# A one-core ConvFFN decoder trunk: the sync engine's loads and stores in the order of the program

## The chip, the cores and the metric

The kernel runs on one core of one Trainium2 chip. A core has a matrix engine (TensorE, "PE" in the profile, with its weight loads as "PEld"), three engines for elementwise work (VectorE "DVE", ScalarE "ACT", GpSimd "POOL"), and a sync engine "SP", which here does nothing but issue transfers. Each engine takes its instructions in one fixed order. An instruction that waits for a semaphore holds up whatever stands behind it on the same engine. Transfers run on 16 DMA engines.

The metric is the device time of one execution in microseconds (us), as the median of several runs. Lower is better.

## The reference

The trunk has two layers, on 1024 positions of 1024 channels in float32. Layer 0 mixes with convolutions, layer 1 with stick-breaking attention. Each layer ends in the gated ConvFFN, which is the part that matters here:

```python
def conv_ffn(h, w_up, dw_w, dw_b, w_down):      # w_up 1024 x 5632, w_down 2816 x 1024
    u = causal_dwconv(h @ w_up, dw_w, dw_b)     # depthwise, width 3
    gate, val = jnp.split(u, 2, axis=-1)
    return (jax.nn.silu(gate) * val) @ w_down

h = rmsnorm(x, ffn_norm_g[layer])
x = x + conv_ffn(h, ...)
```

## The kernel before

Every matrix product in it is made of three: each operand is split into a high part (a cast on ACT) and a low part (a subtraction on DVE), and `mm3` (L641) multiplies high by high, high by low and low by high. Both products of the ConvFFN also use a Strassen-like scheme with seven block products in place of eight, so that sums and differences of blocks are made first.

**Memory.** `Mem` (L48) hands out slots of 128 x 1024 float32 from one list, always the one that was freed longest ago. A transfer into a slot has to wait until every earlier user of that slot is done.

**Up-projection** (`Up`, L153). It runs over 22 blocks `f` of 128 hidden channels. `load(f)` (L174) issues three transfers from SP: half of the value weights (L182, into the slot where a sum will be made), the gate weights (L183) and the value weights (L184). `sums(f)` (L186) makes four weight sums: two negated copies on ACT (L193, L194), then four accumulating transfers from POOL (L199), of which the third reads what the first made. `split1` and `split2` (L202, L210) split weights and sums (casts L628 and L217, subtractions L629 and L218). `block(f)` (L367) starts with `load(f + 2)`, makes the products that are still missing (seven for each block, of 12 matmuls each, with copies L388, L390, L394 and L399 in between), and ends in `post(f)` (L408): the convolution (L817, L819), sigmoid (L420), two multiplications (L421, L422) and `store(f)`. `store` (L427) writes the result to scratch memory `hs`: an even block with one transfer (L434), an odd one, after four sums on DVE (L441), with three (L443). These transfers are issued by SP, but by POOL for the last two blocks.

So the order of the program on SP is: load of block 3, store of block 1, load of block 4, store of block 2, and so on. The load of block `f` stands behind the store of block `f - 3` (the loads of blocks 0 to 2 come before the loop).

**Down-projection** (`Down`, L454). It has 44 steps: four passes `s` over 11 pairs of blocks `i`. A step of the first three passes has 24 matmuls, one of the last pass 12. `load` (L479) issues the transfers of a step: rows of the down weights (L492 in the first pass, L494 in the second, L499 and L500 in the third) and the activations from `hs` (L495). `prep` (L503) makes the differences of weights (L513) and the splits (casts L517, subtractions L518; in the last pass L524 and L525). In the program, `ahead` (L548) puts a step's transfers three steps before its products and its splits two steps before. `run` (L577) also loads halves of the residual `x` (L589, 16 transfers, needed only when a pass ends), adds the products onto it (L571), and calls `tail` for finished rows. In layer 0 the tail is `tail0` (L1560), which loads the weights of the attention (L1160) and stores `x` (L1574). In layer 1 it is `store` (L1549), which writes the output (L1550): in the program, eight of its twelve transfers stand among the loads of the last pass, and four at the end.

**What sets the order.** The program only says what depends on what. The build plays the program through a model of the chip and gives each engine an order of its own, in which an instruction that is free to go may pass one that is not. Only inside `tc.manual_schedule(engines=...)` do the named engines keep the order of the program. Before the change that is used at two places, the start of the first mixer (L924) and the attention (L1454, for PE).

Of the kernel before, what the change touches and what calls it, by code (L numbers as in the profile page):

```python
# [31 lines left out]
NF = DFF // P  # L32
# [586 lines left out]
class Kern:  # L619
# [517 lines left out]
    def ffn(self, l, tail):  # L1137

        up = self.up
        self.banks = deque([b[:, c:c + 512] for b in self.bigs for c in (0, 512)] + self.sms)  # L1140
        up.turn_rest()
        down = Down(self, l, tail)
        for f in range(NF):
            up.block(f)
            if f == NF - 3:
                down.load()
            elif f == NF - 2:
                down.load()
                down.prep()
        up.close()  # L1150
        self.m.give_ht()
        down.run()


    def qkv_load(self, p):
# [466 lines left out]
```

## Time and profile before

| | |
|---|---|
| median of 3 runs | 2364.24 us (2361.4 to 2365.21) |
| the profiled execution, whole | 2360.4 us |
| its span, first to last instruction | 2358.2 us |
| mean granted TensorE clock | 0.982 |
| moved by SP's queue / by POOL's | 238.32 MB / 72.78 MB |

The four stretches that the change reaches are, by the profile's clock: the up-projection of layer 0 from about 385 to 800 us, its down-projection to about 1054 us, the up-projection of layer 1 from about 1710 to 2125 us, and its down-projection to the end.

In rows of a timeline, the columns are the start in us, the duration, engine, line, operation, what is written and read, and the count; in brackets stands the idle time before it and what ended it. SP's rows are issues, not transfers: a row with a count above one begins with the first issue and ends with the last. In the table by stretches, each engine has its busy time and, in brackets, its instructions; then come the granted clock of TensorE, the busy share of the DMA engines, and GB/s.

### The profile page before, as it was taken

Reading aid. Unit: us, or ns where it says so; the run is one execution under the profiler, and the core shown is the slowest. Engines: PE = TensorE matmul, PEld = TensorE weight load, DVE = VectorE, ACT = ScalarE, POOL = GpSimd, SP = SyncE. Lnnn points to the kernel's source line nnn. Section 1 sums busy time; section 2 is a strip of 40 time slices with the busy share of each in tenths; the row PEclk is TensorE's granted clock in tenths of the full one; section 3 lists DMA queues with packets and bytes.
Section 4 is the critical chain, followed back from the end, with each engine's and each line's share of the span. In section 5 each row is a group of like instructions: output and inputs, shape, how many; then the busy total and the mean of one; then the engine's idle time right before and its main releaser. Section 6 shows DMA issues by size and latency. Waiting matters only on the chain. (4 is left out here: it accounts for less than half of the span.)

```text
span 2358.2 us, 29782 instructions
## 1 busy us (share of the span) xinstructions
PE 2250.7 (95%) x11076; PEld 1921.4 (81%) x11076; DVE 1726.9 (73%) x2023; ACT 1263.9 (54%) x1978; POOL 561.3 (24%) x551
## 2 busy tenths in 40 slices
PE   8998999999999989999999999989999999998999
PEld 8876887888888767889999999978778888886777
DVE  6779457877777856556888888887768787786763
ACT  6433336555555423446777676764656555563341
POOL 2221111211111000025555555652221111100000
PEclk9999999999999989999999999989999999999999
DMA  5984046767676863311111110134476676769322
GB/s 173 188 169 105 29 125 148 196 152 188 153 182 164 315 226 103 117 63 28 36 28 37 37 37 10 37 115 149 122 174 159 177 175 167 184 190 391 111 76 76
DMA packets 247827, 313.01 MB, mean 133 GB/s; under 512 B 12557, under 2 KB 170753, under 8 KB 247681
## 3 DMA queue, kind: packets, MB, share of 16 engines
q1 hardware_dynamic: 214977, 238.32, 30.8%
q0 software_dynamic: 32704, 72.78, 17.3%
q8 instruction: 87, 1.43, 0.2%
q14 instruction: 59, 0.48, 0.1%
HBM read 181.14 MB, written 60.82 MB: 103 GB/s over the span
## 5 line engine op out<-in xcount | busy, mean ns | idle before, releaser
L199 POOL DMA_DIRECT2D t<-t x176 | 155.6, 973 | 699.1 <-ACT t L194 285.7
L628 ACT CAST t<-t 128x1024 fp32r<-128x1024 f32 x178 | 185.0, 1048 | 226.7 <-DMA hs<-t 53.3
L629 DVE TENSOR_TENSOR t<-t,t 128x1024 fp32r<-128x1024 f32 x178 | 218.8, 1235 | 100.4 <-ACT t L628 42.3
L819 DVE SCALAR_TENSOR_TENSOR t<-t,cst,t 128x1023 f32<-128x1023 f32 (+1 forms) x184 | 236.1, 1286 | 75.4 <-ACT t L817 69.4
L1273 DVE TENSOR_TENSOR_SCAN t<-t 128x127 f32<-128x127 f32 (+7 forms) x128 | 204.1, 1600 | 7.2 <-ACT t L1264 7.0
L644 PE MATMUL ps1s<-wH,hH 128*128 128x384 f32 x448 | 165.8, 370 | 0.0
L644 PE MATMUL ps0b<-hH,t 128*128 128x512 f32 x396 | 156.3, 396 | 2.7 <-DVE t L1104 1.5
L710 POOL TENSOR_TENSOR stat<-stat,mhalf 128x8 f32<-128x8 f32 (+1 forms) x65 | 80.1, 1233 | 322.9 <-DVE stat L709 320.0
L646 PE MATMUL ps0b<-hH,t 128*128 128x512 f32 x396 | 154.9, 392 | 1.2 <-DVE t L629 1.2
L645 PE MATMUL ps0b<-hL,t 128*128 128x512 f32 x396 | 154.9, 391 | 0.0
L646 PE MATMUL ps1s<-wH,hL 128*128 128x384 f32 x448 | 151.2, 338 | 0.0
L645 PE MATMUL ps1s<-wL,hH 128*128 128x384 f32 x448 | 150.9, 337 | 0.0
L1278 POOL TENSOR_TENSOR t<-t,t 128x639 f32<-128x639 f32 (+1 forms) x64 | 108.5, 1696 | 175.2 <-DVE t L1273 101.0
L817 ACT ACTIVATE t<-t,cst 128x1024 f32<-128x1024 f32 x88 | 109.1, 1240 | 72.9 <-DVE t L392 55.0
L645 PE MATMUL ps2b<-t,t 128*128 128x512 f32 x342 | 133.6, 391 | 3.9 <-DMA t<-t 3.9
L644 PE MATMUL ps2b<-t,t 128*128 128x512 f32 x342 | 133.8, 392 | 3.4 <-ACT t L394 1.6
L646 PE MATMUL ps2b<-t,t 128*128 128x512 f32 x342 | 133.0, 390 | 0.0
L1264 ACT ACTIVATE t<-ps1s 128x512 f32<-128x512 f32 (+1 forms) x192 | 95.5, 497 | 55.2 <-PE ps1s L1260 28.3
L1296 ACT CAST t<-ps1s 128x512 fp32r<-128x512 f32 (+1 forms) x160 | 87.3, 545 | 60.8 <-PE ps1s L1292 53.3
L517 ACT CAST hH<-t 128x1024 fp32r<-128x1024 f32 x64 | 64.9, 1050 | 101.2 <-PE ps2s L645 24.6
L517 ACT CAST hL<-t 128x1024 fp32r<-128x1024 f32 x64 | 65.0, 1051 | 94.8 <-PE ps0bs L645 28.4
L1297 DVE TENSOR_TENSOR t<-ps1s,t 128x512 fp32r<-128x512 f32 (+1 forms) x160 | 100.2, 627 | 21.0 <-ACT t L1296 18.9
(348 smaller groups left out, 6512.2 us busy)
## 6 DMA issues: line engine op xcount, KB each, us to landing
t<-in_ffn_w_up_dram SPq DMA_DIRECT2D x88, 512.0 KB
t<-t POOLq DMA_DIRECT2D x176, 256.0 KB, 4.3
t<-hs SPq DMA_DIRECT2D x66, 512.0 KB
hs<-t SPq DMA_DIRECT2D x60, 512.0 KB
t<-in_ffn_w_down_dram SPq DMA_DIRECT2D x66, 256.0 KB
xd<-t SPq DMA_DIRECT2D x24, 512.0 KB
wr<-in_attn_w_qkv_dram SPq DMA_DIRECT2D x24, 512.0 KB
t<-in_ffn_w_up_dram SPq DMA_DIRECT2D x44, 256.0 KB
```

The lines of the kernel that those rows point to most:

```text
L199: nc.gpsimd.dma_start(out=out, in_=src, accum_op=ALU.add)
L517: nc.scalar.copy(out=r(m.ap(h)), in_=src)
L628: nc.scalar.copy(out=r(m.ap(h)), in_=m.ap(src))
L629: (eng or nc.vector).tensor_tensor(out=r(m.ap(l)), in0=m.ap(src), in1=m.ap(h), op=ALU.subtract)
L644: mm(out=ps, lhsT=sH, rhs=mH, start=start, stop=False, skip_group_check=onto)
L645: mm(out=ps, lhsT=sH, rhs=mL, start=False, stop=False, skip_group_check=onto)
L646: mm(out=ps, lhsT=sL, rhs=mH, start=False, stop=stop, skip_group_check=onto)
L817: nc.scalar.activation(dst, src, AF.Identity, scale=wcols[2], bias=bias)
L819: nc.vector.scalar_tensor_tensor(out=dst[:, s:], in0=src[:, :S - s], scalar=wcols[2 - s], in1=dst[:, s:], op0=ALU.mult, op1=ALU.add)
L1273: self.nc.vector.tensor_tensor_scan(out=rev, data0=rev, data1=rev, initial=1.0, op0=ALU.mult, op1=ALU.bypass)
L1278: self.nc.gpsimd.tensor_tensor(out=B[:, 0:n - 1], in0=B[:, 0:n - 1], in1=K[:, 1:n], op=ALU.mult)
L1297: nc.vector.tensor_tensor(out=r(aL), in0=ps[:, 0:pos], in1=aH, op=ALU.subtract)
```

## The change

The loops over blocks and the down-projection are put in a manual schedule of SP alone. No instruction is added or taken away, and no transfer changes its size or its engine.

```diff
-        for f in range(NF):
-            up.block(f)
-            if f == NF - 3:
-                down.load()
-            elif f == NF - 2:
-                down.load()
-                down.prep()
-        up.close()
-        self.m.give_ht()
-        down.run()
+        with self.tc.manual_schedule(engines={mybir.EngineType.SP}):
+            for f in range(NF):
+                up.block(f)
+                if f == NF - 3:
+                    down.load()
+                elif f == NF - 2:
+                    down.load()
+                    down.prep()
+            up.close()
+            self.m.give_ht()
+            down.run()
```

`ffn` is called once in each layer, so 429 of SP's 565 transfers now stand in the order of the program. `turn_rest`, ahead of the loop, and everything outside `ffn` stay in the build's own order, as do PE, ACT, DVE and POOL everywhere in `ffn`.

## The prediction

> **What bounds it now.** I read the page first, then the table by stretches over the four stages, then PE's waits, and last the timeline of the queues around them.
>
> ```profile
> span 2358.2 us, 29782 instructions
> PE 2250.7 (95%) x11076; PEld 1921.4 (81%) x11076; DVE 1726.9 (73%) x2023; ACT 1263.9 (54%) x1978; POOL 561.3 (24%) x551
> ...
> L629 DVE TENSOR_TENSOR t<-t,t 128x1024 fp32r<-128x1024 f32 x178 | 218.8, 1235 | 100.4 <-ACT t L628 42.3
> ...
> t<-t POOLq DMA_DIRECT2D x176, 256.0 KB, 4.3
> ```
>
> TensorE is the bound, with 2250.7 us of 2358.2. So the change can win only where PE stands still inside the two ConvFFNs. These are the stretches:
>
> ```profile
> 385.00:783.00 398.00, 394.08 (x1722) 323.12 (x1722) 303.41 (x312) 232.16 (x293) 70.82 (x80) 1.00 0.70 173
> 1710.00:2110.00 400.00, 392.71 (x1714) 321.59 (x1714) 301.27 (x310) 231.51 (x293) 70.13 (x80) 1.00 0.70 172
> 807.70:821.40 13.70, 13.67 (x61) 10.99 (x59) 11.23 (x12) 5.10 (x6) 1.61 (x3) 1.00 1.04 402
> 821.40:829.75 8.35, 0.00 (x1) 0.01 (x1) 2.63 (x4) 1.43 (x2) 0.00 (x0) 0.73 1.04 412
> 829.75:834.00 4.25, 4.25 (x10) 3.39 (x11) 1.89 (x2) 0.72 (x1) 0.00 (x0) 0.50 1.02 406
> 849.00:854.30 5.30, 0.03 (x2) 0.01 (x1) 3.65 (x6) 2.15 (x3) 0.00 (x0) 0.83 0.44 158
> 854.30:858.30 4.00, 4.00 (x9) 3.13 (x10) 4.00 (x5) 1.84 (x2) 0.00 (x0) 0.50 0.31 99
> 2149.60:2153.40 3.80, 0.03 (x2) 0.01 (x1) 2.10 (x4) 1.04 (x1) 0.54 (x1) 0.94 1.03 413
> 2153.40:2176.80 23.40, 23.40 (x96) 18.98 (x96) 12.15 (x13) 6.24 (x7) 0.00 (x0) 0.94 1.04 406
> 2176.80:2185.30 8.50, 0.01 (x1) 0.00 (x0) 6.44 (x8) 4.80 (x5) 0.00 (x0) 0.70 0.73 246
> 2185.30:2189.30 4.00, 3.99 (x9) 3.14 (x10) 3.83 (x6) 0.00 (x0) 0.00 (x0) 0.50 0.37 118
> ```
>
> The two up-projections hardly stand still: 398.00 - 394.08 = 3.9 us and 400.00 - 392.71 = 7.3 us. The first pass of each down-projection stops twice: 8.35 and 5.30 us in layer 0, 3.80 and 8.50 us in layer 1, 25.95 us together. And after a stop the clock is halved: 10 matmuls in 4.25 us where 61 take 13.70 us (0.2246 us each), so 4.25 - 10 x 0.2246 = 2.0 us are lost. In the same way 2.0 us go after the second stop, 23.40 - 96 x 0.2246 = 1.8 us after the third and 2.0 us after the fourth, 7.8 us together. The first pass thus holds 25.95 + 7.8 = 33.7 us.
>
> What PE waited for at these stops, and what stood behind that (the first two rows are of layer 0, the last two of layer 1):
>
> ```profile
> PE ps0b L644 <- ACT hH L517: 8.4, 1, 8.4
> DVE t L513 <- DMA t<-in_ffn_w_down_dram: 14.7, 7, 3.0
> PE ps2b L644 <- ACT hH L517: 12.3, 2, 8.5
> DVE t L513 <- DMA t<-in_ffn_w_down_dram: 12.7, 8, 5.1
> ```
>
> PE waits for a cast of an operand, the cast for the differences of weights on DVE (L513), and these for the down weights from memory. The weights are late although the DMA engines are full (share 1.02 to 1.04), so the engines carry something else first. SP's timeline shows what (layer 0):
>
> ```profile
> 790.55 0.86 SPq L589 DMA_DIRECT2D t<-xd  x2
> ...
> 793.14 0.56 SPq L492 DMA_DIRECT2D t<-in_ffn_w_down_dram  x1
> ...
> 797.14 0.33 SPq L500 DMA_DIRECT2D t<-in_ffn_w_down_dram  x1
> ...
> 804.67 2.34 SPq L589 DMA_DIRECT2D t<-xd  x4
> ...
> 809.44 0.33 SPq L492 DMA_DIRECT2D t<-in_ffn_w_down_dram  x1
> ...
> 825.39 5.52 SPq L495 DMA_DIRECT2D t<-hs  x6
> ...
> 837.67 0.33 SPq L492 DMA_DIRECT2D t<-in_ffn_w_down_dram  x1
> ```
>
> L492 is the first pass, needed now. L589 is the residual, needed when a pass ends; L500 at 797 is for the third pass. The build let through whatever had a free slot, and weights of the first pass are still being issued at 837.67, after PE has stopped once for want of them.
>
> **The change, part by part.** It adds and removes no instruction: 429 issues of some 0.4 us change places. Three stretches differ.
>
> (a) First pass of the down-projection. In the program a step brings 512 KB of weights, 512 KB of activations and 256 KB of residual in front of its 24 matmuls (24 x 0.2246 = 5.4 us). That is 1.31 MB in 5.4 us, 243 GB/s, against 402 to 413 GB/s in the full stretches above, so in this order the engines keep ahead. What belongs to later passes comes after the eleven steps. The saving is at most the 33.7 us. What could be late next: SP now stands at the first step whose slot is not free, and some of these slots are freed only by the last block's stores from POOL. The latest such place is where six L495 go in a run at 825.39. It is the ninth step whose weights need that slot; PE stood at 821.40 before the sixth, so without the stop it would reach the ninth at 821.4 + 3 x 5.4 = 837.6. That leaves 12 us for landing and splits, and I cost it at nothing. The second stops of each layer come at a lower DMA share (0.44 and 0.73), and there the order of casts on ACT, which remains the build's own, has its part. Between nothing and 5.30 + 8.50 = 13.8 us may therefore stay; I leave 5 us, nearer to nothing because the weights there were issued late too (837.67).
>
> (b) Up-projection. Here the order costs something: the load of block f now waits for the store of block f - 3, that is for DVE (L422), and everything behind it on SP waits along: the next stores and loads, while DVE, ACT and POOL run on. Rows of SP, POOL and ACT (L388 is the copy that ends the first product with the sums):
>
> ```profile
> 491.63 0.37 SPq L182 DMA_DIRECT2D t<-in_ffn_w_up_dram  x1
> 495.71 0.37 SPq L184 DMA_DIRECT2D t<-in_ffn_w_up_dram  x1
> ...
> 510.94 13.04 SPq L183 DMA_DIRECT2D t<-in_ffn_w_up_dram  x2
> 524.58 0.34 SPq L434 DMA_DIRECT2D hs<-t  x1
> ```
>
> ```profile
> 575.93 2.63 SPq L443 DMA_DIRECT2D hs<-t  x3
> ...
> 640.37 0.32 SPq L434 DMA_DIRECT2D hs<-t  x1
> ```
>
> ```profile
> 502.64 0.87 POOL L199 DMA_DIRECT2D t<-t  x1 [1.69 <-PE ps0b L646]
> ...
> 524.97 1.78 POOL L199 DMA_DIRECT2D t<-t  x2 [7.20 <-ACT t L194]
> ```
>
> ```profile
> 493.94 1.04 ACT L628 CAST t<-t 128x1024 fp32r<-128x1024 f32 x1
> ...
> 551.66 0.58 ACT L388 COPY t<-ps0bs 128x512 f32<-128x512 f32 x1
> ```
>
> ```profile
> 665.00 0.59 ACT L388 COPY t<-ps0bs 128x512 f32<-128x512 f32 x1 [0.92 <-PE ps0bs L646]
> ```
>
> Block 9's loads go at 495.71 to 510.94 now; in program order they go behind the store of block 6 at 524.58, 14 to 29 us later. How long they need: block 8's last load at 491.63, its third accumulation issued at 502.64, landing 4.3 us later (the page's median), cast and subtraction 1.04 and 1.24 us: 17.6 us. Block 9's own chain is slower, because POOL waited for ACT: from 510.94 to the two issues from 524.97, their landing and the split, some 21.6 us. The product starts 12 x 0.2246 = 2.7 us before the copy. So block 9 has 551.66 - 2.7 - 524.58 = 24.4 us, less 1 us for the three issues: 1.8 us to spare by the slow chain, 5.8 by the fast. Block 15, the tightest of layer 0, has 665.00 - 2.7 - 640.37 = 21.9 us less 1: late by 0.7 us by the slow chain, 3.3 to spare by the fast. Even blocks have more (their products come later, at a pace of one block in 84 x 0.2246 = 18.9 us). I take the slow chain and two such places in a layer at about 1 us each: 4 us. Bounds: nothing, and 2.5 us for every odd block from 5 on, 9 x 2 x 2.5 = 45 us.
>
> (c) The end of layer 1. The last pass's loads of steps 3 to 10 now stand behind and among eight output stores, which wait for the residual sums:
>
> ```profile
> 2319.70 2.05 DVE L571 TENSOR_TENSOR t<-ps2b,t 128x512 f32<-128x512 f32 x3 [11.65 <-PE ps2b L646]
> ...
> 2331.69 2.66 DVE L525 TENSOR_TENSOR t<-t,t 128x512 fp32r<-128x512 f32 x4 [6.54 <-ACT t L524]
> 2342.14 0.69 DVE L571 TENSOR_TENSOR t<-ps2b,t 128x512 f32<-128x512 f32 x1 [7.79 <-PE ps2b L646]
> ```
>
> Eight sums of 0.68 us end at 2325; then 16 subtractions of 0.665 us, from about 2328 on as the loads land, end at 2338.6; PE needs the last of them one product (0.7 us) before 2342.14. It fits by 2.8 us: nothing. Without that cushion it costs up to 5 us. Layer 0's tail waits for the attention's weights in the same way, but PE has the projections of finished rows to do meanwhile: nothing.
>
> Sum: -33.7 + 5 + 4 + 0 = -24.7 us. The profiled execution would go from 2360.4 to 2335.7. It lies 3.8 us under the median of the runs, so for the median 2364.2 - 24.7 = 2339.5 us.
>
> [...]
>
> **Rivals.** *The wait for the store reaches PE.* Each odd block of the up-projection is late, because its loads hang on DVE's L422 three blocks earlier. For: block 15's -0.7 us, and stores and loads now land together. Against: three blocks take 57 us, while load, sums and split (22.6 us) and the way from a product to the last store (block 9: from 549.0 to 578.6, the end of its row, 29.6 us) take 52, so a block that is late once makes the next ones fit. At 2.5 us a block it costs 45 us; the balance turns at (33.7 - 5) / 18 = 1.6 us a block. Time: 2364.2 - 28.7 + 45 = 2380.5. *The stop only moves.* SP stands before a slot held by the last block, later loads bunch behind it, and the first pass loses its 33.7 us at another step. For: the run at 825.39 above. Against: the 12 us. Time: 2364. *It does little.* The build plans the other engines around the new order and puts their work off in the same measure; half the gain goes: 2352.
>
> **Chances.** The forecast with its half-gain neighbour 0.62 (own range 2328 to 2356), the stop only moves 0.12, the wait reaches PE 0.26. A measurement of this kernel tells about 0.2% (4.7 us) from no change, so faster 0.62, same 0.12, slower 0.26. The range goes from 2326 (the 33.7 us and 4 of the 11 us idle in the up-projections) to 2382 (the first rival); beyond are its worse forms.
>
> **What would show it.** Right in (a): no stop over 3 us in the first passes, L589 spread one to a step, DMA share below 1. Right in (b): PE's idle time between 385 and 783 stays under 8 us. Wrong: products waiting for L628 or L629 of the sums in odd blocks, POOL's L199 waiting for the up weights. Wrong in (c): PE idle after the third pass, waiting for L525. If the first pass still stops, the row to look at is the cast that ended it: behind a late weight it is SP, behind another cast it is the build's order on ACT.

## The result, and the profile after

The changed kernel is slower: a median of 2391.18 us (2388.74 to 2395.48, 4 runs) against 2362.82 us for the kernel before (2359.23 to 2365.21, 4 runs on the same chip). The ratio is 1.0123, with a 95% interval of 1.0103 to 1.0144, so some 28 us are lost where the forecast had 25 us gained. Line numbers from L1143 on are one higher in the changed kernel.

The page of the changed kernel, profiled in an execution of 2391.28 us:

```profile
PE 2254.3 (94%) x11076; PEld 1917.7 (80%) x11076; DVE 1728.5 (72%) x2023; ACT 1263.0 (53%) x1978; POOL 561.1 (23%) x551
...
L199 POOL DMA_DIRECT2D t<-t x176 | 155.3, 931 | 788.3 <-DMA t<-in_ffn_w_up_dram 414.8
L628 ACT CAST t<-t 128x1024 fp32r<-128x1024 f32 x178 | 185.5, 1047 | 287.1 <-DMA t<-t 127.9
L629 DVE TENSOR_TENSOR t<-t,t 128x1024 fp32r<-128x1024 f32 x178 | 219.3, 1238 | 159.4 <-ACT t L628 142.8
```

and the same groups of the kernel before (its L629 stands in the prediction: 42.3 us behind ACT's L628), in the view by lines:

```profile
L628 ACT CAST t<-t 128x1024 fp32r<-128x1024 f32 x178 | 185.0, 1048 | 226.7 <-DMA hs<-t 53.3 <-PE ps0b L646 30.8 <-DVE t L422 29.9
...
L199 POOL DMA_DIRECT2D t<-t x176 | 155.6, 973 | 699.1 <-ACT t L194 285.7 <-DMA t<-in_ffn_w_up_dram 145.9 <-DMA t<-t 108.9
```

No engine has more than 4 us more to do. What changed is what they wait for. POOL, which starts the accumulations (L199), waited 145.9 us for the up weights before; now it waits 414.8 us for them. ACT's casts (L628) now wait 127.9 us for the accumulations ("t<-t"), a releaser that isn't among the first three before, and DVE waits for ACT. Lateness goes down the whole chain.

The stretches of the changed kernel: the up-projection of layer 0 and its first pass, then those of layer 1.

```profile
385.00:800.00 415.00, 385.24 (x1629) 310.64 (x1628) 286.85 (x292) 219.23 (x277) 67.73 (x78) 0.97 0.64 152
800.00:889.70 89.70, 88.95 (x393) 73.18 (x392) 73.46 (x80) 42.11 (x46) 3.74 (x6) 1.00 0.79 284
1700.99:2150.00 449.01, 417.60 (x1772) 338.61 (x1773) 315.25 (x345) 238.56 (x302) 74.04 (x85) 0.97 0.62 148
2150.00:2233.50 83.50, 80.36 (x351) 65.31 (x350) 67.65 (x75) 40.42 (x44) 2.22 (x4) 1.00 0.76 273
```

The two halves of the forecast came out on opposite sides. The first pass of layer 0 now runs without a stop: PE is busy 88.95 of 89.70 us, at a granted clock of 1.00. But the up-projection, which idled 3.9 us before, idles 415.00 - 385.24 = 29.8 us, and its clock fell to 0.97, some 3% of 385 us more. Layer 1 shows the same: 449.01 - 417.60 = 31.4 us idle in the up-projection, and a first pass whose waits come to 3.1 us in all, the longest 2.0 us.

How a late load reaches PE can be read at one stop, that of 3.03 us at 555.29. First the issues of SP, then of POOL, then ACT, then PE:

```profile
535.08 0.34 SPq L434 DMA_DIRECT2D hs<-t  x1
535.58 0.37 SPq L182 DMA_DIRECT2D t<-in_ffn_w_up_dram  x1
...
536.66 0.53 SPq L184 DMA_DIRECT2D t<-in_ffn_w_up_dram  x1
546.90 1.64 SPq L443 DMA_DIRECT2D hs<-t  x3
548.65 1.19 SPq L182 DMA_DIRECT2D t<-in_ffn_w_up_dram  x1
...
551.68 2.27 SPq L184 DMA_DIRECT2D t<-in_ffn_w_up_dram  x1
```

```profile
542.97 1.78 POOL L199 DMA_DIRECT2D t<-t  x2 [13.20 <-DMA t<-in_ffn_w_up_dram]
546.67 0.87 POOL L199 DMA_DIRECT2D t<-t  x1 [1.92 <-DMA t<-t]
```

```profile
553.71 1.04 ACT L628 CAST t<-t 128x1024 fp32r<-128x1024 f32 x1 [9.43 <-DMA t<-t]
554.66 0.58 ACT L394 COPY t<-ps0bb 128x512 f32<-128x512 f32 x1
```

```profile
555.29 0.79 PE L644 MATMUL ps0bb<-t,t 128*128 128x512 f32 x1 [3.03 <-ACT t L394]
```

The loads of block 9 (L182 to L184) go right behind the store at 535.08, as the program has it. POOL waits 13.20 us for them. Its third accumulation for block 9 goes at 546.67; from 546.90 on SP gets the next stores and block 10's loads away, and the accumulation lands only at 553.7, after 7.0 us. ACT stands 9.43 us before the cast of that sum. Behind the cast, in ACT's fixed order, stands L394, a copy that empties one of PE's banks for block 8. PE has work that needs no late operand, but it needs that bank. So this stop is *not* the product with the late sum; it is a copy for an earlier block.

Not every stop is of this kind. These are the two largest of PE's waits in the up-projection of each layer of the changed kernel (total, times, longest):

```profile
PE ps0bs L644 <- ACT t L628: 8.7, 4, 3.6
PE ps0b L644 <- ACT t L399: 6.7, 2, 6.4
...
PE ps2b L644 <- ACT t L394: 9.4, 4, 4.2
PE ps2b L644 <- ACT t L399: 7.0, 1, 7.0
```

Over all such rows of both layers, PE waits 41.4 us for something that empties a bank (L351, L388, L390, L392, L394, L399) and 20.4 us for the cast or the subtraction of an operand that its next product uses (L628, L629).

### The profile page after: what moved, and what is told of

Its sections match the earlier page's. It is cut to its first block, busy times and chain, and to the rows that moved or that the text cites. A ratio compares the mean times of both kernels' runs of the same rounds, so it can differ in the third digit from the quotient of the medians.

```text
span 2389.5 us, 29615 instructions
## 1 busy us (share of the span) xinstructions
PE 2254.3 (94%) x11076; PEld 1917.7 (80%) x11076; DVE 1728.5 (72%) x2023; ACT 1263.0 (53%) x1978; POOL 561.1 (23%) x551
## 5 line engine op out<-in xcount | busy, mean ns | idle before, releaser
L199 POOL DMA_DIRECT2D t<-t x176 | 155.3, 931 | 788.3 <-DMA t<-in_ffn_w_up_dram 414.8
L628 ACT CAST t<-t 128x1024 fp32r<-128x1024 f32 x178 | 185.5, 1047 | 287.1 <-DMA t<-t 127.9
L629 DVE TENSOR_TENSOR t<-t,t 128x1024 fp32r<-128x1024 f32 x178 | 219.3, 1238 | 159.4 <-ACT t L628 142.8
L645 PE MATMUL ps0b<-hL,t 128*128 128x512 f32 x396 | 155.6, 393 | 0.0
L645 PE MATMUL ps1s<-wL,hH 128*128 128x384 f32 x448 | 150.8, 337 | 0.0
L644 PE MATMUL ps2b<-t,t 128*128 128x512 f32 x342 | 136.8, 401 | 12.4 <-ACT t L394 9.4
L645 PE MATMUL ps2b<-t,t 128*128 128x512 f32 x342 | 135.9, 398 | 0.0
L646 PE MATMUL ps2b<-t,t 128*128 128x512 f32 x342 | 134.7, 396 | 0.0
L644 PE MATMUL ps2b<-hH,t 128*128 128x512 f32 x256 | 102.6, 401 | 17.1 <-ACT t L399 7.0
```

Of the source, the lines that this page charges most:

```text
L199: nc.gpsimd.dma_start(out=out, in_=src, accum_op=ALU.add)
L628: nc.scalar.copy(out=r(m.ap(h)), in_=m.ap(src))
L629: (eng or nc.vector).tensor_tensor(out=r(m.ap(l)), in0=m.ap(src), in1=m.ap(h), op=ALU.subtract)
L644: mm(out=ps, lhsT=sH, rhs=mH, start=start, stop=False, skip_group_check=onto)
L645: mm(out=ps, lhsT=sH, rhs=mL, start=False, stop=False, skip_group_check=onto)
L646: mm(out=ps, lhsT=sL, rhs=mH, start=False, stop=stop, skip_group_check=onto)
```

## The experiments

All were timed against the kernel before on the same chip (its medians there lie between 2361.38 and 2362.65 us), and each ratio is to that. Theory A is that SP's order wins in the down-projection and loses in the up-projection, because loads there stand behind stores.

**The down-projection alone.**

```diff
-        with self.tc.manual_schedule(engines={mybir.EngineType.SP}):
-            for f in range(NF):
+        for f in range(NF):
...
-            down.run()
+        with self.tc.manual_schedule(engines={mybir.EngineType.SP}):
+            down.run()
```

> SP keeps the order of the program in the down-projection alone; the loop over blocks is back in the build's order. Theory A (the stops of the first pass come from SP's order there, and the loss of the change is in the up-projection alone): the first passes have no stop over 3 us, the up-projections look as before, and about 33 us are gained: 2363 - 33 = 2330, between 2325 and 2340. Rival (the first pass only ran through because the up-projection before it was late and left the transfers time): the stops come back and the time is 2355 to 2365.

Measured: 2322.41 us, ratio 0.9831 (0.9814 to 0.9848), that is 39.0 us faster. Up-projection and first pass of layer 0, then of layer 1, by stretches:

```profile
380.00:780.00 400.00, 395.06 (x1722) 324.52 (x1723) 305.77 (x317) 235.19 (x296) 71.05 (x80) 0.99 0.68 170
780.00:854.00 74.00, 73.51 (x323) 60.27 (x322) 59.53 (x66) 33.86 (x36) 2.20 (x4) 1.00 0.76 284
...
2090.00:2165.00 75.00, 74.32 (x327) 60.99 (x326) 61.32 (x66) 34.71 (x38) 2.22 (x4) 1.00 0.71 266
```

Theory A holds and the rival falls: with the up-projection as before, the first passes still run through (0.5 and 0.7 us idle). The gain is some 6 us over the 33 expected. PE's waits for the residual sums (L571) in the two down-projections fell from 5.6 to 3.2 us, which is 2.4 us of it; where the rest comes from was not traced.

**The loop over blocks alone.** The loop stays in the manual schedule, `up.close()` to `down.run()` come out of it.

> SP keeps the order of the program in the loop over blocks alone; the down-projection is back in the build's order. Theory A: the up-projections lose what the two traces show, 32 us in layer 0 and 37 us in layer 1, and the first passes stop again for 34 us: 2363 + 69 = 2432, between 2415 and 2440. Rival (a late up-projection lets the first pass run through): about 2391 to 2400.

Measured: 2425.66 us, ratio 1.0268 (1.0253 to 1.0283), 64.3 us slower. PE's waits in the first pass, layer 0 and then layer 1:

```profile
PE ps0b L644 <- ACT hL L517: 6.5, 1, 6.5
PE ps0b L644 <- ACT hH L517: 5.7, 1, 5.7
...
PE ps2b L644 <- ACT hH L517: 7.3, 1, 7.3
PE ps2b L644 <- ACT hL L517: 6.0, 2, 3.2
```

The first passes stop again, for 25.5 us against 25.95 before, though the up-projection is late. So they ran through in the changed kernel because of SP's order in them. The two parts add up: 64.3 - 39.0 = 25.3 us, against some 28 us for the whole change.

**The loads one store earlier**, with all of the change in place:

```diff
-        if f + 2 < NF and f + 2 not in self.raw:
-            self.load(f + 2)
...
             self.split2(f + 1)
+        if f + 3 < NF:
+            self.load(f + 3)
         self.post(f, g, v)
```

> The changed kernel, but load(f + 3) is called ahead of post(f), so the load of block f stands behind the store of block f - 4 and not f - 3, some 19 us earlier. Theory A (the loads are late because they stand behind a store): the stops of 3 to 7 us in the up-projection go, of its 69 us at most 15 stay, 2330 to 2345. Rival B (not the lateness but the bunching of three loads and a store with the accumulations, or the order that the build plans for the other engines around a fixed SP): the bunch stays, and the time is 2380 to 2395.

Measured: 2330.14 us, ratio 0.9864 (0.9849 to 0.9878). The up-projections of layers 0 and 1, by stretches:

```profile
385.00:790.00 405.00, 393.19 (x1699) 320.01 (x1698) 297.78 (x306) 228.23 (x288) 71.06 (x80) 0.99 0.68 164
1685.00:2100.00 415.00, 407.68 (x1789) 333.91 (x1788) 316.38 (x339) 242.85 (x307) 73.74 (x84) 1.00 0.69 167
```

and the casts in its view by lines:

```profile
L628 ACT CAST t<-t 128x1024 fp32r<-128x1024 f32 x178 | 184.5, 1047 | 167.1 <-DMA t<-t 46.3 <-PE ps0b L646 31.6 <-DVE t L858 16.1
```

Of the 64 us, 61 go (2391 to 2330), with SP's order as fixed as before and the same transfers in the same bunches. The casts' wait for accumulations falls from 127.9 to 46.3 us. It is the lateness. Rival B falls, and the traces say the same of bunching: of the 152 accumulations of blocks 3 to 21, counted from issue to landing, 36 took over 6 us in the kernel before, 12 in the changed one and 21 here. Long accumulations were most common in the kernel before, whose up-projections idled 3.9 and 7.3 us; one shows only where no time is left. At 555.29 the two met: the 7.0 us of that accumulation are 3.6 us over the changed kernel's median of 3.4, about as much as the stop.

**One store earlier still** (`load(f + 4)` ahead of `post(f)`, and `load(3)` in block 0 too).

> The changed kernel with the loads called one more block earlier (load(f + 4) ahead of post(f); load 3 in block 0 too), so the load of block f stands behind the store of block f - 5. With f - 3 the time is 2391, with f - 4 it is 2330. Theory A (a load waits for a store only where the store is late for it): the rest of the stops goes as far as slots allow, 2320 to 2330, near the 2322 of the down-projection alone. Rival (what is left is bunching or the build's plan around a fixed SP): 2328 to 2340. If slots are the next wait, loads stand on slots and it is slower than 2330.

Measured: 2511.09 us, ratio 1.0635 (1.0619 to 1.0650), 180 us beyond theory A's range: the last case named, slots, and far worse than the other two. SP's and POOL's timeline (in this kernel L437 is the store L434, L183 the load L182, L200 the accumulation L199):

```profile
498.15 0.34 SPq L437 DMA_DIRECT2D hs<-t  x1
506.30 0.37 SPq L183 DMA_DIRECT2D t<-in_ffn_w_up_dram  x1
```

```profile
513.80 0.88 POOL L200 DMA_DIRECT2D t<-t  x1 [24.59 <-DMA t<-in_ffn_w_up_dram]
```

The load doesn't go right behind the store at 498.15 but 8.15 us later: its slot isn't free, since for 7.8 us SP waits for a product of PE that reads what is there (L648, which is L645). A block earlier means three more slots held, and SP, in order, now stands on slots with the next store behind the load. POOL then waits 24.59 us for weights, part of it because the store at 498.15 was itself late: SP had waited 19.9 us for DVE's result there.

**Even or odd blocks alone early.** The same move of the call, for `f` odd (loads of even blocks) or `f` even; the others keep `load(f + 2)` at the head of the block.

```diff
+        if f + 3 < NF and f % 2 == 1:
+            self.load(f + 3)
         self.post(f, g, v)
```

> The changed kernel, with load(f + 3) called ahead of post(f) for the loads of even blocks alone; odd blocks' loads stay behind the store of f - 3. My forecast said that odd blocks are the tight ones and even blocks have more time; by that, little is gained: 2380 to 2391. By the changed kernel's trace the stops that end on an even block's sums (4, 10, 12, 18) are some 30 of 50 us: about 2350, between 2340 and 2365. If one early load in two is enough slack for both: 2330 to 2340.

> The same for the loads of odd blocks alone; even blocks' loads stay behind the store of f - 3, an odd block's, which waits for the four sums (L441) besides. By my forecast (odd blocks are tight): most of the loss goes, 2330 to 2345. By the changed kernel's trace (stops that end on the sums or the weights of blocks 9, 15 and 17 are some 20 of 50 us): about 2363, between 2355 and 2375.

Measured: even early 2348.35 us, ratio 0.9940 (0.9918 to 0.9961); odd early 2367.59 us, ratio 1.0016 (1.0003 to 1.0029). Against the changed kernel 43 and 24 us go, 67 together, where both at once gave 61. PE's waits in the up-projection of layer 0, even early and then odd early (L630 is the cast L628):

```profile
PE ps0bs L646 <- ACT t L630: 7.2, 6, 2.6
```

```profile
PE ps0b L646 <- ACT t L394: 11.9, 5, 3.4
```

Both kinds of blocks were late, and the even ones cost more. Their loads stand behind an odd block's store, which waits for four sums besides; that this is the reason was not tested.

**The stores on POOL**, so that no load on SP stands behind a store (`eng = nc.gpsimd` in `store`).

> The changed kernel, but all stores of the up-projection are issued by POOL, so no load on SP stands behind a store. Theory A: the loads go when their slots are free, as in the kernel before, and the time is 2330 to 2345, if POOL's accumulations are not held by the stores that now wait on POOL. Rival B (the order that the build plans for ACT and PE around a fixed SP): 2380 to 2395. If POOL is the new place of the wait: 2360 to 2400, with accumulations (L199) waiting behind stores.

Measured: 2362.88 us, ratio 1.0008 (0.9995 to 1.0020): the time of the third case, a new wait on POOL. POOL now stands before the stores of even blocks until DVE has their result, and its accumulations stand behind them (layer 0):

```profile
POOL hs L434 <- DVE t L422: 33.7, 8, 8.4
```

A second kind of wait was not named. POOL, then ACT, at a stop of 4.39 us (473.18):

```profile
461.78 0.80 POOL L443 DMA_DIRECT2D hs<-t  x1
468.49 0.86 POOL L199 DMA_DIRECT2D t<-t  x1 [5.91 <-issue]
```

```profile
469.95 1.04 ACT L628 CAST t<-t 128x1024 fp32r<-128x1024 f32 x1 [9.34 <-DMA hs<-t]
...
472.56 0.56 ACT L394 COPY t<-ps0bb 128x512 f32<-128x512 f32 x1
```

The cast wants the slot of a stored tile and waits 9.34 us for that store, the one issued at 461.78, which landed 8.1 us after its issue. Again L394 stands behind the cast. Why this store took so long was not tested.

**The casts of the sums on POOL**, with the loads as late as in the changed kernel. This tests how lateness reaches PE.

```diff
-        s34 = k.split(s34)
+        s34 = k.split(s34, cast=k.nc.gpsimd.tensor_copy)
...
-        nc.scalar.copy(out=r(m.ap(h)), in_=m.ap(src))
+        (cast or nc.scalar.copy)(out=r(m.ap(h)), in_=m.ap(src))
```

> The changed kernel, but the casts (L628) of the weight sums are made by POOL and not by ACT, so that a cast that waits for its accumulation no longer holds up ACT's copies out of PE's banks (L351, L388, L390, L394, L399). The loads are as late as before. Theory C (of the 69 us, most are PE waiting for copies that stand behind late casts on ACT): in the changed kernel's waits PE waits 15 us in layer 0 and 24 us in layer 1 for these copies; they go, and the time is 2391 - 39 = 2352, between 2342 and 2362. Rival (the sums are late themselves, so PE stops at the product with the sums as long as it stopped at the copies before): 2380 to 2400.

Measured: 2368.7 us (2361.0 to 2373.32), ratio 1.0027 (1.0014 to 1.0040): 22 us of the expected 39, between the two. DVE's and PE's waits in layer 0:

```profile
DVE t L629 <- POOL t L628: 31.3, 16, 5.2
```

```profile
PE ps0bb L644 <- DVE t L392: 7.0, 3, 2.7
```

ACT is freed, but now the subtraction L629 waits on DVE for POOL's cast, and behind it stands L392, which takes a bank's content too.

**Casts and subtractions of the sums on POOL.** The subtractions go there as well.

> The changed kernel with the casts (L628) and the subtractions (L629) of the weight sums on POOL, so that neither ACT nor DVE stands behind an accumulation. With the casts alone on POOL the time was 2369 and PE still waited 12 us for DVE's L392, which takes a bank's content behind a subtraction of a late sum. Theory C (the late sums reach PE through the engines that empty its banks, ACT and DVE, since these keep their order): these 12 us go too, 2350 to 2362. Rival (POOL takes their place: the next block's accumulations stand behind casts and subtractions, and a POOL subtraction is slower than DVE's, so the sums come later still): 2370 to 2400.

Measured: 2433.86 us, ratio 1.0295 (1.0270 to 1.0320): the rival, and worse than it said. The groups in the view by lines:

```profile
L629 POOL TENSOR_TENSOR t<-t,t 128x1024 fp32r<-128x1024 f32 x88 | 240.3, 2732 | 49.1 <-issue 31.3 <-DVE t L441 5.5 <-DVE t L819 5.1
...
L629 DVE TENSOR_TENSOR t<-t,t 128x1024 fp32r<-128x1024 f32 x90 | 116.5, 1304 | 70.4 <-ACT t L628 55.6 <-DMA t<-t 14.0 <-POOL t L629 0.4
```

A subtraction takes 2.73 us on POOL against 1.30 on DVE, and the issues of accumulations stand behind it in POOL's order. The lateness can be moved from engine to engine; in no place tried was it free. How much of the 64 us would go if no copy stood behind a late cast, these two runs don't settle, since each of them made another engine wait; 22 us are the part that one move took away.

**The first pass alone** in the program's order (11 steps of `run`, the rest in the build's order).

> SP in the order of the program in the first pass of the down-projection alone (11 of its 44 steps, each with the loads of the step three ahead); all the rest is in the build's order. Theory A (the gain is that the first pass's weights no longer stand behind loads of later passes): as with the whole down-projection, 2318 to 2330. Rival (the order in the later passes, or the end of a layer, has its part): 2335 to 2350.

Measured: 2339.53 us, ratio 0.9908 (0.9891 to 0.9925), 21.9 us of the 39. This isn't the clean test that it was meant to be. SP's timeline in layer 0:

```profile
820.16 0.33 SPq L494 DMA_DIRECT2D t<-in_ffn_w_down_dram  x1
822.72 0.33 SPq L500 DMA_DIRECT2D t<-in_ffn_w_down_dram  x1
...
828.92 0.33 SPq L492 DMA_DIRECT2D t<-in_ffn_w_down_dram  x1
```

The region keeps the order of its own transfers, but what comes after it in the program is still let in between: weights of the second and third pass (L494, L500) ahead of the first pass's L492 at 828.92. The first passes still stop, in layer 0 and in layer 1:

```profile
PE ps0b L649 <- ACT hL L517: 3.8, 1, 3.8
...
PE ps2b L649 <- ACT hH L517: 4.8, 1, 4.8
```

So some 22 us come with the order among the first pass's own loads. Of the other 17, the two stops that are left are 8.6 us, before what a lower clock behind them costs (0.65 from 839 to 843 us, at the end of the first stop and behind it; behind the second it was not read). The one in layer 0 is late weights again: DVE's L513 waits 12.9 us for them between 790 and 850 us. The rest may be this too, or the order in the later passes; the run doesn't separate the two.

**The down-projection alone, with the early loads.** The best two edits together.

> SP in the order of the program in the down-projection alone, and load(f + 3) called ahead of post(f) as in the run with the early loads; the loop over blocks is in the build's order. The down-projection alone gave 2322. Theory A: in the build's order the loads pass the stores anyway, so the place of the call matters little: 2318 to 2328. If the earlier call also gives the build other slots and an earlier start of the sums, up to 8 us of stops in the up-projections go: 2314.

Measured: 2321.40 us, ratio 0.9834 (0.9816 to 0.9852), the same as the down-projection alone. In the build's order a load passes the stores anyway, so the place of its call hardly counts. The fastest kernel of the study is thus the change on `down.run()` only, some 39 us under the kernel before and 69 under the change as made.

## Why the prediction was wrong

- **What bounds the kernel, and where it stops** (right). The four stops of the first passes are as read; with only the loop in the program's order they are still there.
- **(a) First pass** (right in mechanism, too small in size). Forecast: 33.7 us less 5 us left over, with 33.7 us as the most. Measured: 39.0 us (35.9 to 43.9 by the interval) with the down-projection alone, above that bound; only 2.4 us of the excess are traced, to L571. The share of the DMA engines in the first pass is 0.79, below 1 as expected. The 5 us kept back for the build's order of casts were not needed: both second stops went too. The six L495 no longer go in a run. SP does stand before slots (it issues nothing between 828.06 and 842.14 in the changed kernel), but the first passes don't stop for it, so *the stop only moves* is out.
- **(b) Up-projection** (the step that failed). Forecast: 4 us, at most 45. Measured: 64.3 us, outside the bounds. Three sentences of that step were wrong. First, "while DVE, ACT and POOL run on": they didn't. The late chain runs through POOL, ACT and DVE, each with its fixed order (around the stop at 555.29 they stood 13.20, 9.43 and 7.18 us), and behind a late cast stand the copies that empty PE's banks. I named what stands behind the store on SP, but not what stands behind the load's consumers on three other engines. Second, I set the deadline of the sums at their own product (for block 9 at 551.66 - 2.7) and found 1.8 us to spare. An earlier deadline is the place of their cast in ACT's order: at 553.71 it stands ahead of L394 of block 8, which PE needed at once. Such waits for banks are 41 us against 20 us for operands in the changed kernel, and 28 against 27 with the loop alone in the program's order, so operands were late at their own product as well. The chain to that product was also sized too short: I gave its accumulations the median of 4.3 us, but the two issued from 524.97 landed 6.9 and 7.6 us after their issue. With these the same sum has block 9 some 1 us late, as an estimate, and not 1.8 us early. Third, "even blocks have more": they held the larger part, 43 us against 24. I worked out blocks 9 and 15, both odd, and judged the others by their products' times alone.
- **"A block that is late once makes the next ones fit"** (wrong). The stops come back in both layers all through the loop. Spread over 2 x 19 blocks, 64.3 us are 1.7 us a block, of either kind.
- **(c) The end of layer 1** (right). With this stretch in the program's order PE waits 0.7 us in all from the third pass to the end, for L571; L525 does not appear.
- **The rivals.** *The wait for the store reaches PE* is what happened, though not in the form described: it priced odd blocks only, at 45 us where the loop cost 64.3, and its 2380.5 us were 11 us short. Of its signs in "what would show it", POOL's L199 waits 414.8 us for the up weights, and products wait for L628 and L629 (in which blocks was not traced), but the larger waits are for copies out of banks, which were not among the signs.

So one term of the sum was mis-sized, by 60 us: the price of taking away lead from a load whose consumers share engines with work that PE needs sooner. That the sum missed by 52 us (2339.5 against 2391.2) and not by more is luck, since the first pass gave 10 us more than forecast.

## What to carry to other kernels

When a change makes an operand later, look for the first instruction that will wait for it on each in-order engine, and price what stands behind that instruction there; the product that uses the operand can be a later deadline than the one that counts. A fixed order on SP's queue gained 39 us here in the stage whose transfers had filled the DMA engines (share 1.02 to 1.04 around the first stop of each layer in the kernel before) and whose order of need is known, and it cost 64 us in the stage where it tied loads to stores, so decide it by stage. In this kernel one position in the program was worth 61 us, and one more cost 181: between a store and a slot there was room for one block of lead.

## What the runs showed of the hardware

An accumulating transfer of 256 KB took 3.4 us from issue to landing at the median on the changed kernel's page; one took 7.0 us when three stores and three loads were issued within some 7 us behind it. The issues on SP were longer too in such a bunch: 0.37 to 0.53 us each for the loads at 535.58, and 1.19 to 2.27 us for those at 548.65, which follow three stores.

Here a stop's length alone didn't say whether the clock was halved. Behind a stop of 2.89 us in the changed kernel it was 0.50; behind one of 2.94 us, in the kernel with the casts on POOL, it was 1.00:

```profile
2009.47 0.79 PE L644 MATMUL ps2s<-hH,t 128*128 128x512 f32 x1 [2.89 <-ACT t L628]
```

```profile
2009.47:2011.50 2.03, 2.03 (x5) 1.64 (x6) 2.00 (x3) 2.00 (x3) 0.51 (x1) 0.50 0.97 163
```

```profile
433.27 0.50 PE L644 MATMUL ps0bs<-hH,t 128*128 128x512 f32 x1 [2.94 <-POOL t L628]
```

```profile
433.27:435.30 2.03, 1.96 (x7) 1.34 (x8) 2.03 (x2) 0.99 (x1) 0.00 (x0) 1.00 1.03 296
```

The second row is the stretch behind the stop of 2.89 us, the last that behind the stop of 2.94 us; the third figure from the end is the clock.
